# Forgetting heads that read their bias as loaded strips, and a top-k spread over the heads, in a hybrid decoder layer

## The chip, the cores and the metric

The kernel runs on one core of one Trainium2 chip. The metric is the device time of one execution in microseconds (us), as the median of the runs shown. PE is the tensor engine, PEld its weight loads, DVE the vector engine, ACT the scalar engine, POOL the GpSimd engine, and SP the engine whose queue issues most of the DMA transfers.

## The reference, cut

One layer over 512 positions of width 1024: a half-step SwiGLU block, then attention in two branches of 8 heads of 64, then a second half-step SwiGLU block. Branch A ("forgetting", heads 0 to 7) adds to its logits the difference of running sums of log-forget gates. Branch B ("sparse", heads 8 to 15) keeps, for each query, the 128 causal keys with the highest indexer scores. Both work in blocks of 128 queries.

```python
def fox_attention(q, k, v, log_f):
    cum = jnp.cumsum(log_f, axis=1).transpose(0, 2, 1)
    ...
        logits = jnp.einsum('bqhd,bkhd->bhqk', q[:, start:end], k[:, :end]).astype(jnp.float32) * scale
        logits = logits + cum[:, :, start:end, None] - cum[:, :, None, :end]
        logits = jnp.where(kpos <= qpos, logits, NEG_INF)
        p = jax.nn.softmax(logits, axis=-1).astype(v.dtype)
        outs.append(jnp.einsum('bhqk,bkhd->bqhd', p, v[:, :end]))

def dsa_attention(q, k, v, q_idx, k_idx, w_idx, rel_bias):
    ...
        score = jnp.einsum('bqhk,bqh->bqk', s_idx, w[:, start:end])
        score = jnp.where(causal[None], score, NEG_INF)
        _, sel = lax.top_k(score, topk)
        ...
        logits = logits + bias.transpose(0, 3, 1, 2)
        logits = jnp.where(valid[:, None], logits, NEG_INF)
        p = jax.nn.softmax(logits, axis=-1).astype(v.dtype)
```

## The kernel before

Every float32 operand of a large product is split into a high and a low half (tiles named h and l: wh and wl of weights, xh and xl of activations, ph and pl of softmax weights), and a product is three matmuls, or two where the halves of one side are stacked in one tile. `load_w` loads a weight tile over SP (ra, rb and rc in turn), ACT casts it to wh, and DVE subtracts it into wl.

The order of PE's instructions is the order of the code; that of the other engines is set by the compiler's scheduler, which fills gaps by its own estimates and keeps that order on each queue. The attention part stands in the middle of the kernel, between the two SwiGLU blocks. `Products` deals out projection matmuls (the units fk1, fq1, fv1 and so on) between the steps of the heads, by a fixed table FILL, so that PE always has work.

A head has four steps, s = 0 to 3, one query block each, the longest first: step s treats block i = 3 - s, with n = 128 (i + 1) keys. `softmax_block` takes the bias, lets PE form the logits (ps_qk, two banks of PSUM, with the scale's sign turned so that a minimum stands for a maximum), and DVE adds the bias and takes the minimum mn in one instruction (the line of `p<-ps_qk`). ACT takes the exponential and its sum, DVE the reciprocal rs, POOL scales p by it. `value_step`, which runs one head later, transposes p on PE (pt), splits it on ACT and DVE (ph, pl) and multiplies it with the values (po) one step after that.

For a forgetting head, `get_bias` loads the head's row of running sums (`cum_rows`, in DRAM), the same row to all 128 partitions, as one tile cb of 512 columns, of two in turn. For each block POOL makes a new tile b = cb - cum of the query (ncum, one value for each partition) and then sets the columns of the diagonal square that lie ahead of the query to 1e30. A sparse head's b is the selection (sc, 0 or 1e30) less a loaded table of relative positions.

The selection is made on DVE in `topk_steps`: 16 rounds over three score tiles (sc of 256, 384 and 512 columns), each a MAX of 8 values and a MATCH_REPLACE, and three last instructions; 99 steps in all. `topk_run(n)` adds n to a debt and takes a step for each whole unit. It is called after each small piece of projection ahead of the heads with TOPK_PRE, and twice in each block of the heads with TOPK_BEAT; at the end of head 7 what is left is taken at once. The tile sg holds small projections (forget logits, values and weights of the indexer) and cum the running sums.

Of the kernel before, what the change touches and what calls it, by code (L numbers as in the profile page):

```python
# [12 lines left out]
F32 = mybir.dt.float32  # L13
F32R = mybir.dt.float32r
AF = mybir.ActivationFunctionType
OP = mybir.AluOpType
# [3 lines left out]
P = 128  # L20
T = 512
NT = T // P
# [8 lines left out]
FILL_IX = 0.5  # L31
TOPK_PRE, TOPK_BEAT = 1.25, 1

# [3 lines left out]
H = 8  # L37
# [3 lines left out]
BIG = 1e30  # L41
S_W = 208
# [13 lines left out]
def tile_hybrid_layer(ctx: ExitStack, tc: tile.TileContext, a: dict):  # L56
    nc = tc.nc
    V, S, G, PE = nc.vector, nc.scalar, nc.gpsimd, nc.tensor
# [6 lines left out]
    small = ctx.enter_context(tc.tile_pool(name="small", bufs=4))  # L65
# [13 lines left out]
    for _ in range(WARM):  # L79
# [6 lines left out]
                    pattern=[[1, P]], channel_multiplier=-1)  # L86
    cpos = const.tile([P, P], F32, name="cpos")
# [781 lines left out]
    with (tc.tile_pool(name="mix", bufs=1) as mp, ExitStack() as att_ctx,  # L869
# [5 lines left out]
        kept = mp_dram.tile([P, 5, T], F32, name="kept")  # L875
        sg = at.tile([P, NT, S_W - 128], F32, name="sg")
        sd = [at.tile([P, NT, 2, DH], F32, tag="cb", bufs=2, name="sd") for _ in range(2)]
        dkh = at.tile([P, T], F32R, name="dkh")
        dkl = at.tile([P, T], F32R, name="dkl")
        dvv = at.tile([P, NT, P], F32R, name="dvv")  # L880
        cum = at.tile([P, NT, H], F32, name="cum")
        ncum = at.tile([P, NT, H], F32, name="ncum")
        dram = att_ctx.enter_context(tc.tile_pool(name="dram", bufs=1, space=bass.MemoryType.DRAM))
# [263 lines left out]
        def forget():  # L1147
# [25 lines left out]
            PE.matmul(pc[:, :NT * H], trin, lf.rearrange("p t h -> p (t h)"), start=True, stop=False)  # L1173
            PE.matmul(pc[:, :NT * H], ones, before.rearrange("p t h -> p (t h)"), start=False, stop=True)
            V.tensor_copy(cum, pc[:, :NT * H].rearrange("p (t h) -> p t h", t=NT))
            V.tensor_scalar(ncum, cum, -1.0, None, op0=OP.mult)
            yield
# [110 lines left out]
        def get_k(g):  # L1288
# [15 lines left out]
            return out  # L1304

        def get_bias(g):
            cb = at.tile([P, T], F32, tag="cb", bufs=2, name="cb")
            nc.sync.dma_start(cb, cum_rows[g:g + 1, :].to_broadcast([P, T]) if g < H else a["rel"][g - H])

            def bias(i):  # L1310
                n = P * (i + 1)
                b = tmp_tile("b")
                if g < H:
                    G.tensor_scalar(b[:, :n], cb[:, :n], 1.0, ncum[:, i, g:g + 1], op0=OP.mult, op1=OP.add)
                    G.affine_select(out=b[:, i * P:n], in_=b[:, i * P:n], compare_op=OP.is_ge, fill=BIG, base=0,
                                    pattern=[[-1, P]], channel_multiplier=1)
                else:
                    G.tensor_sub(b[:, :n], sc[i] if i else cpos, cb[:, T - n:T])
                return b[:, :n]
            return bias  # L1320
# [6 lines left out]
        for step in range(30):  # L1327
            prod.run(MM, upto["fv0"])
            topk_run(TOPK_PRE)
            if step == 5:  # L1330
                nk = get_k(0)
            if step == 10:
                next(later[1], 0)
            if step == 15:
                nq = get_q(0)
            if step == 24:
                nb = get_bias(0)
        prod.finish(upto["fv0"])
# [37 lines left out]
        for g in range(2 * H):  # L1376
            q, k, bias = nq, nk, nb
            probs[g] = [None] * NT
            st = [small.tile([P, NT], F32, tag=nm, name=nm) for nm in ("mn", "rs")]
            for s in range(NT):  # L1380
# [6 lines left out]
                if g + 1 < 2 * H:  # L1387
                    if s == 0:
                        nb = get_bias(g + 1)
                    if s == 0 and g % 2:  # L1390
                        nk = get_k(g + 1)
                    if s == 1 and g % 2:
                        nq = get_q(g + 1)
# [131 lines left out]
```

## Time and profile before

| | |
|---|---|
| runs, us | 1044.01, 1043.91, 1044.5; median 1044.01 |
| profiled execution, us | 1043.44, span 1041.7 |
| granted clock | 1.0 |
| DVE, ACT, POOL busy | 82%, 64%, 25% of the span |
| stretch with the forgetting heads | about 427 to 533 us |

An engine's busy time in a row of a stretch comes with the count of its instructions in brackets. In rows in order of time the first number is the start from the span's beginning, the second the length; a bracket at the end holds the idle time of the engine before the row and what ended it. SPq is SP's queue of transfers. Matmuls overlap: the next starts before the one ahead is over.

### The profile page before, as it was taken

The numbers are of one execution on the slowest core, as the hardware profiler recorded it, in microseconds if no ns is written. First come the engines' busy times: TensorE is split into PE (matmuls) and PEld (weight loads), VectorE is DVE, ScalarE is ACT, GpSimd is POOL, SyncE is SP. The second block draws the span as 40 slices with busy tenths as digits, with TensorE's granted clock in tenths as the row PEclk, the third lists the DMA queues.
The fourth block names the chain that finished last, engine by engine and source line by source line (L and its number), as shares of the span: only waits on it lengthen the run. The fifth ranks groups of instructions, "written<-read, shape, count | busy, mean of one in ns | idle before, by whom it ended". The sixth has DMA issues, their size and how long they took to land.

```text
span 1041.7 us, 19489 instructions
## 1 busy us (share of the span) xinstructions
PE 1027.9 (99%) x7424; PEld 960.6 (92%) x7424; DVE 851.7 (82%) x1405; ACT 668.8 (64%) x1118; POOL 256.6 (25%) x324
## 2 busy tenths in 40 slices
PE   9999999999999999999999999999999999999998
PEld 8889999999999999989887788888889999999998
DVE  6897888897989779977868765853987888988887
ACT  6547765865787765567767665433736865875783
POOL 1100111120121124285867552000100210111111
PEclk9999999999999999999999999999999999999999
DMA  7444755666567367633314311532553665567554
GB/s 257 108 152 120 158 161 132 150 163 175 124 142 185 113 166 190 182 97 93 86 57 132 119 54 52 181 112 81 131 164 96 146 150 177 129 162 192 131 128 132
DMA packets 57341, 142.66 MB, mean 137 GB/s; under 512 B 6424, under 2 KB 15768, under 8 KB 57248
## 3 DMA queue, kind: packets, MB, share of 16 engines
q1 hardware_dynamic: 39600, 110.21, 34.1%
q0 software_dynamic: 17504, 30.94, 16.6%
q8 instruction: 58, 0.95, 0.4%
q10 hardware_dynamic: 144, 0.27, 0.1%
q14 instruction: 35, 0.29, 0.1%
HBM read 104.94 MB, written 3.42 MB: 104 GB/s over the span
## 4 chain that ended last, share of the span: by engine, by line
PE 89%; DVE 5%; POOL 3%; issue 2%; DMA 1%; ACT 1%; POOLq 0%; DVEq 0%; ACTq 0%
PE pB L155 5%; PE pB L157 5%; PE pB L156 5%; PE ps_f L155 3%; PE pA L155 3%; PE pA L157 3%; PE pA L156 3%; PE ps_f L157 3%; PE ps_f L156 3%; PE dB L157 2%; PE dB L155 2%; PE dB L156 2%; PE ps_t L157 2%; PE ps_t L155 2%; PE ps_t L156 2%; PE dA L156 2%
## 5 line engine op out<-in xcount | busy, mean ns | idle before, releaser
L123 ACT CAST wh<-s 128x1024 fp32r<-128x1024 f32 (+1 forms) x90 | 86.8, 965 | 66.8 <-PE pC L156 31.5
L130 DVE TENSOR_TENSOR wl<-s,wh 128x1024 fp32r<-128x1024 f32 (+1 forms) x90 | 100.4, 1116 | 19.9 <-ACT wh L123 19.9
L155 PE MATMUL ps_t<-wh,xh 128*128 128x256 f32 (+1 forms) x288 | 81.2, 282 | 0.0
L157 PE MATMUL ps_t<-wh,xl 128*128 128x256 f32 (+1 forms) x288 | 80.4, 279 | 0.0
L156 PE MATMUL ps_t<-wl,xh 128*128 128x256 f32 (+1 forms) x288 | 80.3, 279 | 0.0
L155 PE MATMUL pB<-tbh,wh 128*128 128x256 f32 x288 | 79.5, 276 | 0.0
L156 PE MATMUL pB<-tbl,wh 128*128 128x256 f32 x288 | 79.5, 276 | 0.0
L157 PE MATMUL pB<-tbh,wl 128*128 128x256 f32 x288 | 79.5, 276 | 0.0
L249 POOL DMA_DIRECT2D b<-gu x12 | 10.4, 864 | 220.3 <-DVE rb L449 89.4
L155 PE MATMUL ps_f<-xh,wh 128*128 128x512 f32 (+1 forms) x152 | 59.0, 388 | 0.0
L157 PE MATMUL ps_f<-xh,wl 128*128 128x512 f32 (+1 forms) x152 | 57.9, 381 | 0.0
L156 PE MATMUL ps_f<-xl,wh 128*128 128x512 f32 (+1 forms) x152 | 57.7, 380 | 0.0
L1242 ACT ACTIVATE p<-p,mn 128x512 f32<-128x512 f32 (+1 forms) x64 | 36.1, 564 | 29.5 <-DVE mn L1240 29.2
L155 PEld LDWEIGHTS ps_t<-wh,xh 128*128 128x128 f32 x288 | 54.5, 189 | 0.5
L156 PEld LDWEIGHTS ps_t<-wl,xh 128*128 128x128 f32 x288 | 54.4, 189 | 0.5
L157 PEld LDWEIGHTS ps_t<-wh,xl 128*128 128x128 f32 x288 | 54.4, 189 | 0.2 <-DVE xl L168 0.2
L157 PEld LDWEIGHTS pB<-tbh,wl 128*128 128x128 f32 x288 | 54.1, 188 | 0.0
L156 PEld LDWEIGHTS pB<-tbl,wh 128*128 128x128 f32 x288 | 54.1, 188 | 0.0
L155 PEld LDWEIGHTS pB<-tbh,wh 128*128 128x128 f32 x288 | 54.1, 188 | 0.0
L1244 POOL TENSOR_SCALAR p<-p,rs 128x512 f32<-128x512 f32 (+1 forms) x64 | 39.2, 615 | 58.9 <-DVE rs L1243 53.5
L575 POOL DMA_DIRECT2D gx<-e x20 | 23.9, 1241 | 119.4 <-ACT wh L123 99.9
L1256 DVE TENSOR_TENSOR pl<-pt,ph 128x512 fp32r<-128x512 f32 (+1 forms) x64 | 31.0, 485 | 17.7 <-ACT ph L1255 17.5
(406 smaller groups left out, 4195.9 us busy)
## 6 DMA issues: line engine op xcount, KB each, us to landing
rf<-in_w_pair_dram SPq DMA_DIRECT2D x15, 512.0 KB, 4.1
rc<-in_w_pair_dram SPq DMA_DIRECT2D x12, 512.0 KB, 3.6
re<-in_w_pair_dram SPq DMA_DIRECT2D x12, 512.0 KB, 3.6
rd<-in_w_pair_dram SPq DMA_DIRECT2D x12, 512.0 KB, 4.0
rb<-in_w_pair_dram SPq DMA_DIRECT2D x12, 512.0 KB, 4.3
gx<-e POOLq DMA_DIRECT2D x22, 256.0 KB, 4.3
ra<-in_w_pair_dram SPq DMA_DIRECT2D x9, 512.0 KB, 3.8
rd<-in_w_halves_dram SPq DMA_DIRECT2D x12, 384.0 KB, 3.7
```

Source lines behind the costliest of these rows:

```text
L123: S.copy(wh[:, :f], raw[:, :f])
L130: V.tensor_sub(wl[:, :f], raw[:, :f], wh[:, :f].bitcast(F32))
L155: PE.matmul(out, lh, rh, start=start, stop=False, **more)
L156: PE.matmul(out, lh, rl, start=False, stop=False, **more)
L157: PE.matmul(out, ll, rh, start=False, stop=stop, **more)
L249: G.dma_start(l, src, accum_op=OP.add)
L575: G.dma_start(xa[:, d:d + 2, HT:], t["e"][part], accum_op=OP.add)
L1242: S.activation(p, p, AF.Exp, bias=mn, scale=-1.0, accum_out=rs)
L1244: G.tensor_scalar(p, p, rs, 1.0, op0=OP.mult, op1=OP.mult)
L1256: V.tensor_sub(pl[:, sl], pt[:, sl], ph[:, sl].bitcast(F32))
```

## The change

Four strips of running sums are loaded for each forgetting head, one for each block, 128 (i + 1) columns wide, and POOL writes the 1e30 into the diagonal square of the strip itself. DVE adds the strip to the logits as it is. The query's own sum is left out: it is one number for a whole row of logits, and the softmax does not change with it. So ncum and POOL's 32 subtractions are gone, and SP has 32 loads in the place of 8. Strips 3 and 2 take turns in the two cb buffers, strip 3 of the next head loaded at step 1 and strip 2 at step 2; strips 1 and 0 share one buffer (that of sg) and are loaded at step 0 of their own head. The top-k takes 1.1 and 0.25 steps a call in the place of 1.25 and 1.

```diff
--- before.py
+++ after.py
@@ -29,7 +29,7 @@
 FILL = (2.1, 2.3, 2.0, 2.0, 1.7, 1.7, 1.7, 1.7, 2.0, 2.0, 1.9, 1.9, 1.9, 1.9, 2.0, 2.2)
 FILL_LAST = 0.8
 FILL_IX = 0.5
-TOPK_PRE, TOPK_BEAT = 1.25, 1
+TOPK_PRE, TOPK_BEAT = 1.1, 0.25
 
 ADDING = range(6, 16)
 MM = 0.64
@@ -873,13 +873,11 @@
         rt = rb = None
         tn, fv, iq, pA, ga, gb = {}, {}, [], [], [], []
         kept = mp_dram.tile([P, 5, T], F32, name="kept")
-        sg = at.tile([P, NT, S_W - 128], F32, name="sg")
+        sg = at.tile([P, 3 * P], F32, tag="sg", name="sg")[:, :NT * (S_W - 128)].rearrange("p (t c) -> p t c", t=NT)
         sd = [at.tile([P, NT, 2, DH], F32, tag="cb", bufs=2, name="sd") for _ in range(2)]
         dkh = at.tile([P, T], F32R, name="dkh")
         dkl = at.tile([P, T], F32R, name="dkl")
         dvv = at.tile([P, NT, P], F32R, name="dvv")
-        cum = at.tile([P, NT, H], F32, name="cum")
-        ncum = at.tile([P, NT, H], F32, name="ncum")
         dram = att_ctx.enter_context(tc.tile_pool(name="dram", bufs=1, space=bass.MemoryType.DRAM))
         cum_rows = dram.tile([H, T], F32, name="cum_rows")
         wi = at.tile([P, NT, H], F32, name="wi")
@@ -1172,8 +1170,8 @@
             pc = psum.tile([P, T], F32, tag="pt", bufs=2, name="pc")
             PE.matmul(pc[:, :NT * H], trin, lf.rearrange("p t h -> p (t h)"), start=True, stop=False)
             PE.matmul(pc[:, :NT * H], ones, before.rearrange("p t h -> p (t h)"), start=False, stop=True)
+            cum = small.tile([P, NT, H], F32, tag="cr", bufs=1, name="cum")
             V.tensor_copy(cum, pc[:, :NT * H].rearrange("p (t h) -> p t h", t=NT))
-            V.tensor_scalar(ncum, cum, -1.0, None, op0=OP.mult)
             yield
             ps = psum.tile([P, T], F32, tag="pt", bufs=2, name="ps_ct")
             for t in range(NT):
@@ -1303,19 +1301,31 @@
                 out.append(k)
             return out
 
+        def causal_rows(g, i):
+            if i:
+                strip = at.tile([P, T] if i > 1 else [P, 3 * P], F32, tag="cb" if i > 1 else "sg",
+                                bufs=2 if i > 1 else 1, name="cb")
+            else:
+                strip = strips[1][:, 2 * P:]
+            n = P * (i + 1)
+            nc.sync.dma_start(strip[:, :n], cum_rows[g:g + 1, :n].to_broadcast([P, n]))
+            G.affine_select(out=strip[:, i * P:n], in_=strip[:, i * P:n], compare_op=OP.is_ge, fill=BIG, base=0,
+                            pattern=[[-1, P]], channel_multiplier=1)
+            strips[i] = strip
+
+        strips = {}
+
+        def forget_bias(i):
+            return strips[i][:, :P * (i + 1)]
+
         def get_bias(g):
             cb = at.tile([P, T], F32, tag="cb", bufs=2, name="cb")
-            nc.sync.dma_start(cb, cum_rows[g:g + 1, :].to_broadcast([P, T]) if g < H else a["rel"][g - H])
+            nc.sync.dma_start(cb, a["rel"][g - H])
 
             def bias(i):
                 n = P * (i + 1)
                 b = tmp_tile("b")
-                if g < H:
-                    G.tensor_scalar(b[:, :n], cb[:, :n], 1.0, ncum[:, i, g:g + 1], op0=OP.mult, op1=OP.add)
-                    G.affine_select(out=b[:, i * P:n], in_=b[:, i * P:n], compare_op=OP.is_ge, fill=BIG, base=0,
-                                    pattern=[[-1, P]], channel_multiplier=1)
-                else:
-                    G.tensor_sub(b[:, :n], sc[i] if i else cpos, cb[:, T - n:T])
+                G.tensor_sub(b[:, :n], sc[i] if i else cpos, cb[:, T - n:T])
                 return b[:, :n]
             return bias
 
@@ -1334,7 +1344,8 @@
             if step == 15:
                 nq = get_q(0)
             if step == 24:
-                nb = get_bias(0)
+                for i in (3, 2, 1, 0):
+                    causal_rows(0, i)
         prod.finish(upto["fv0"])
 
 
@@ -1374,7 +1385,7 @@
             return upto["dq1"] if g < 6 else upto["ga7"] if 4 * g + s < 4 * 9 + 2 else len(units)
 
         for g in range(2 * H):
-            q, k, bias = nq, nk, nb
+            q, k, bias = nq, nk, forget_bias if g < H else nb
             probs[g] = [None] * NT
             st = [small.tile([P, NT], F32, tag=nm, name=nm) for nm in ("mn", "rs")]
             for s in range(NT):
@@ -1385,8 +1396,14 @@
                 softmax_block(g, NT - 1 - s, q, k, bias, probs[g], st)
                 prod.run(FILL[g] / 2, limit(g, s))
                 if g + 1 < 2 * H:
-                    if s == 0:
+                    if s and g + 1 < H:
+                        for i in ((), (3,), (2,), ())[s]:
+                            causal_rows(g + 1, i)
+                    if s == 0 and g + 1 >= H:
                         nb = get_bias(g + 1)
+                    if s == 0 and 0 < g < H:
+                        for i in (1, 0):
+                            causal_rows(g, i)
                     if s == 0 and g % 2:
                         nk = get_k(g + 1)
                     if s == 1 and g % 2:
```

The scheduler sets a new order on DVE, ACT, POOL and SP; PE's is the same. In the rows below, p,mn<-ps_qk is the block's instruction, MAX and MATCH_REPLACE are top-k steps, fv belongs to the values, rs is a reciprocal, kl and st belong to the next heads' K and Q.

First place, DVE at head 0's first two blocks, before and now:

```order
L1014 SCALAR_TENSOR_TENSOR fv<-ps_t,rstd,fv 128x4x64
L1189 MAX m_5331<-sc_4155 128x8
L1191 MATCH_REPLACE sc_4154<-m_5310,sc_4154 128x384
L1189 MAX m_5354<-sc_4153 128x8
L1240 ISA p,mn<-ps_qk,b 128x512
L1240 ISA mn 128x1
L150 TENSOR_TENSOR wl<-rc,wh 128x1024
L1191 MATCH_REPLACE sc_4155<-m_5331,sc_4155 128x512
L1014 SCALAR_TENSOR_TENSOR fv<-ps_t,rstd,fv 128x4x64 x2
L1189 MAX m_5363<-sc_4154 128x8
L1191 MATCH_REPLACE sc_4153<-m_5354,sc_4153 128x256
L1240 ISA p,mn<-ps_qk,b 128x384
```

```order
L1012 SCALAR_TENSOR_TENSOR fv<-ps_t,rstd,fv 128x4x64 x2
L1238 ISA p,mn<-ps_qk,cb 128x512
L1238 ISA mn 128x1
L1189 MATCH_REPLACE sc_4151<-m_5378,sc_4151 128x256
L150 TENSOR_TENSOR wl<-rc,wh 128x1024
L1012 SCALAR_TENSOR_TENSOR fv<-ps_t,rstd,fv 128x4x64
L1241 RECIPROCAL rs<-rs 128x1
L1238 ISA p,mn<-ps_qk,cb 128x384
L1238 ISA mn 128x1
L1012 SCALAR_TENSOR_TENSOR fv<-ps_t,rstd,fv 128x4x64
```

Behind the first block stood four steps ahead of the second, and there are fewer in front of the first too; one is left between them.

Second place, DVE at the end of head 2 and the start of head 3 (the blocks of 128 and 512 columns), before and now:

```order
L1243 RECIPROCAL rs<-rs 128x1
L1240 ISA p,mn<-ps_qk,b 128x128
L1240 ISA mn 128x1
L1240 ISA p,mn<-ps_qk,b 128x512
L1240 ISA mn 128x1
L150 TENSOR_TENSOR wl<-rb,wh 128x1024
L1256 TENSOR_TENSOR pl<-pt,ph 128x128
L1243 RECIPROCAL rs<-rs 128x1 x2
```

```order
L1241 RECIPROCAL rs<-rs 128x1
L1254 TENSOR_TENSOR pl<-pt,ph 128x256
L1238 ISA p,mn<-ps_qk,cb 128x128
L1238 ISA mn 128x1
L896 TENSOR_SCALAR ss<-ss 128x8
L1241 RECIPROCAL rs<-rs 128x1
L1238 ISA p,mn<-ps_qk,cb 128x512
L1238 ISA mn 128x1
L150 TENSOR_TENSOR wl<-rb,wh 128x1024
L1189 MATCH_REPLACE sc_4151<-m_5940,sc_4151 128x256
L1254 TENSOR_TENSOR pl<-pt,ph 128x128
L1241 RECIPROCAL rs<-rs 128x1
```

The reciprocals of head 2's last blocks stood behind the split wl<-rb, two of them at once; now that of the block of 128 stands ahead of head 3's first block and of the split, and a replace stands behind the split.

Third place, DVE at the end of head 7, before from its block of 256 columns on, now from the row behind it:

```order
L1240 ISA p,mn<-ps_qk,b 128x256
L1240 ISA mn 128x1
L1276 TENSOR_TENSOR oAl<-o,oAh 64x512
L1240 ISA p,mn<-ps_qk,b 128x128
L1240 ISA mn 128x1
L1256 TENSOR_TENSOR pl<-pt,ph 128x256
L1243 RECIPROCAL rs<-rs 128x1 x2
L1036 TENSOR_TENSOR ga<-ps_f,rb 128x512
```

```order
L1187 MAX m_6910<-sc_4153 128x8
L1187 MAX m_6942<-sc_4151 128x8
L1187 MAX m_6945<-sc_4152 128x8
L1254 TENSOR_TENSOR pl<-pt,ph 128x384
L1274 TENSOR_TENSOR oAl<-o,oAh 64x512
L1189 MATCH_REPLACE sc_4153<-m_6910,sc_4153 128x512
L918 SCALAR_TENSOR_TENSOR st<-ps_q,gq,st 64x512
L1189 MATCH_REPLACE sc_4151<-m_6942,sc_4151 128x256
L1241 RECIPROCAL rs<-rs 128x1
L1189 MATCH_REPLACE sc_4152<-m_6945,sc_4152 128x384
L1254 TENSOR_TENSOR pl<-pt,ph 128x256
L1238 ISA p,mn<-ps_qk,cb 128x128
```

Three MAX now stand between the block and the next pl, and three MATCH_REPLACE ahead of the one behind that; the rest of the top-k (one MAX and replace and the three last instructions) follows behind the block of 128, ahead of head 8's first block.

## The prediction

> **What bounds the kernel now.** I read the page first, then busy time by stretch, then the rows of PE in order of time where it stood idle, then who had kept it waiting.
>
> ```profile
> span 1041.7 us, 19489 instructions
> PE 1027.9 (99%) x7424; PEld 960.6 (92%) x7424; DVE 851.7 (82%) x1405; ACT 668.8 (64%) x1118; POOL 256.6 (25%) x324
> PE 89%; DVE 5%; POOL 3%; issue 2%; DMA 1%; ACT 1%; POOLq 0%; DVEq 0%; ACTq 0%
> ...
> 427.00:457.00 30.00, 26.77 (x217) 25.63 (x216) 29.43 (x86) 19.74 (x41) 16.91 (x28) 1.00 0.43 131
> 457.00:533.00 76.00, 72.45 (x533) 67.63 (x532) 57.38 (x137) 57.02 (x128) 59.69 (x90) 1.00 0.29 85
> ```
>
> PE is busy for 99% of the span, so only PE's own holes can be won. The two stretches (columns: width, PE, PEld, DVE, ACT, POOL, clock, DMA share, GB/s) hold the eight forgetting heads: heads 0 and 1 in 427 to 457, heads 2 to 7 in 457 to 533. PE lacks 3.23 us in the first and 3.55 in the second. In the first DVE is full (29.43 of 30), in the second it has a quarter free. A softmax block goes PE logits, DVE sum with the bias and minimum, ACT exponential, DVE reciprocal, POOL scaling; four blocks later it goes PE transpose, ACT high half, DVE low half pl, PE product po. PE fills the time between with projections, so a late link costs it nothing until a transpose finds p unscaled or a po finds pl unmade. The holes one by one, with the idle time and what ended it in brackets:
>
> ```profile
> 442.11 0.66 PE L1251 MATMUL pt<-ident,p 128*128 128x128 f32 x4 [0.71 <-POOL p L1244]
> 447.12 0.55 PE L1251 MATMUL pt<-ident,p 128*128 128x128 f32 x3 [1.09 <-DVE pl L1256]
> 451.53 0.44 PE L1251 MATMUL pt<-ident,p 128*128 128x128 f32 x2 [0.77 <-DVE pl L1256]
> 455.84 0.39 PE L1262 MATMUL po<-pl,fv 128*128 128x256 f32 x1 [0.66 <-DVE pl L1256]
> 473.08 0.66 PE L1251 MATMUL pt<-ident,p 128*128 128x128 f32 x4 [1.43 <-POOL p L1244]
> 504.68 0.41 PE L1251 MATMUL pt<-ident,p 128*128 128x128 f32 x2 [0.62 <-DVE rs L1243]
> 513.64 0.50 PE L1261 MATMUL po<-ph,fv 128*128 128x512 f32 x1 [0.27 <-ACT o L1271]
> 520.23 0.39 PE L1262 MATMUL po<-pl,fv 128*128 128x256 f32 x1 [0.78 <-DVE pl L1256]
> 523.36 0.65 PE L1251 MATMUL pt<-ident,p 128*128 128x128 f32 x4 [0.23 <-POOL p L1244]
> ...
> 399.81 0.28 PE L156 MATMUL ps_t<-wl,xh 128*128 128x256 f32 x1
> 399.93 0.28 PE L157 MATMUL ps_t<-wh,xl 128*128 128x256 f32 x1
> ```
>
> The last two rows show that a busy matmul runs 0.28 us while the next starts 0.12 after it, so a hole costs about 0.16 more than its idle time. Four holes in the first stretch: 3.23 + 4 x 0.16 = 3.87 us. Five in the second: 3.33 + 0.80 = 4.13. About 8.0 us is all that this change can win on PE, whose own instructions stand in the same order before and after.
>
> **Fewer top-k steps in front.**
>
> ```profile
> 427.00:457.00 30.00, 14.68 (x40) 0.00 (x0) 1.00 0.43 131
> L1189 DVE MAX8 m<-sc x48: 408/562/723, 379.4 to 450.3; 128x8 f32<-128x256 f32 x16, 128x8 f32<-128x384 f32 x16, 128x8 f32<-128x512 f32 x16
> L1191 DVE MATCH_VALUE_LOAD sc<-m,sc x48: 64/86/121, 380.9 to 453.1; 128x8 f32 x48
> L1191 DVE MATCH_REPLACE8 sc<-m,sc x48: 399/552/719, 380.9 to 453.2; 128x256 f32<-128x256 f32 x16, 128x384 f32<-128x384 f32 x16, 128x512 f32<-128x512 f32 x16
> ...
> 427.56 0.40 PE L929 MATMUL ps_qk<-kl,st 128*128 128x512 f32 x1
> 430.51 0.68 DVE L1240 CUSTOM_DVE_ANT_0 p<-ps_qk,b 128x512 f32<-128x512 f32 x1
> ```
>
> The first row is the same stretch for the tile sc alone: 14.68 us of DVE's 29.43 are top-k. A step is a MAX (0.56) or a load and replace (0.09 + 0.55), 0.60 in the mean. Head 0's first logits are there at 427.96; DVE comes to them at 430.51, 2.55 late, and the holes at 447, 451 and 455 still wait for its pl. In the rows of order of the first place, and counted on, 78 of the 99 steps stood ahead of the first softmax block and all 99 ahead of the ninth block; now it is 73 and 77. So 22 steps x 0.60 = 13.2 us leave a stretch in which DVE was some 2.5 us late, and it needs about 16 us of 30 (29.43 - 13.2). The reciprocals of head 0, which stood two and three steps behind their exponentials, then reach POOL blocks ahead of the transpose at 442. All four holes should close: I take 3.8. Ends: 3.87, and 2.0 if a late weight load holds ACT and DVE instead (below).
>
> Of the 22 steps, 11 now lie singly in blocks 10 to 30 and 11 in a lump. The single ones, 11 x 0.6 = 6.6 us, enter a DVE that is 75% busy (57.38 of 76). Most fall into its idle time; I charge 0.8, one more hole like that at 520.23, between 0 and 4.
>
> The lump (third place) stands on both sides of head 7's last block, because the sparse heads' bias needs the finished selection. Rows for it:
>
> ```profile
> 527.18 0.27 PE L929 MATMUL ps_qk<-kl,st 128*128 128x256 f32 x1
> 529.75 0.34 PE L1262 MATMUL po<-pl,fv 128*128 128x384 f32 x1
> 532.74 0.39 PE L1262 MATMUL po<-pl,fv 128*128 128x256 f32 x1
> ...
> L1240 DVE CUSTOM_DVE_ANT_0 p<-ps_qk,b 128x512 f32<-128x512 f32 (+3 forms) x32 | 15.5, 486 | 3.4 <-POOL b L1315 2.8 <-PE ps_qk L929 0.2
> L1256 DVE TENSOR_TENSOR pl<-pt,ph 128x512 fp32r<-128x512 f32 (+3 forms) x27 | 13.2, 489 | 3.6 <-ACT ph L1255 3.5
> L1276 DVE TENSOR_TENSOR oAl<-o,oAh 64x512 fp32r<-64x512 f32 x6 | 6.3, 1047 | 0.1
> L920 DVE SCALAR_TENSOR_TENSOR st<-ps_q,gq,st 64x512 fp32r<-64x512 f32 x8 | 6.0, 750 | 1.1 <-ACT st L919 0.9
> L1318 POOL TENSOR_TENSOR b<-sc,cb x24: 738/1021/2286, 527.4 to 626.3; 128x512 f32<-128x512 f32 x8, 128x384 f32<-128x384 f32 x8, 128x256 f32<-128x256 f32 x8
> ```
>
> Walk it in before's times: logits ready at 527.45, block 0.58 (to 528.03), three MAX 1.69 (529.7), pl 0.49 (530.2): PE wanted that pl at 529.75, 0.5 late. Then oAl 1.05, replace 0.64, st 0.75, replace 0.64, rs 0.16, replace 0.64, pl 0.49: 534.6, where PE, itself 0.5 late, wants it at 533.2: 1.4 late. After the last step POOL forms the bias of head 8's first block (1.0 to 1.3) with DVE waiting for it; two banks for logits cover that but for some 0.1. I charge 2.0, between 0 (the scheduler's order fits the gaps) and 3.5 (the bias wait comes through whole).
>
> **Loaded strips instead of a bias made on POOL.**
>
> ```profile
> L1314 POOL TENSOR_SCALAR b<-cb,ncum x32: 368/539/1543, 425.3 to 527.0; 128x512 f32<-128x512 f32 x8, 128x384 f32<-128x384 f32 x8, 128x256 f32<-128x256 f32 x8, 128x128 f32<-128x128 f32 x8
> 437.92 1.22 DVE L150 TENSOR_TENSOR wl<-ra,wh 128x1024 fp32r<-128x1024 f32 x1
> 469.87 2.42 DVE L150 TENSOR_TENSOR wl<-rb,wh 128x1024 fp32r<-128x1024 f32 x1
> 470.15 1.04 POOL L1004 TENSOR_TENSOR kn<-kn,rh 128x512 f32<-128x512 f32 x1
> 472.65 1.05 POOL L1244 TENSOR_SCALAR p<-p,rs 128x128 f32<-128x128 f32 x2 [1.45 <-DVE rs L1243]
> ```
>
> POOL loses 32 x 0.54 = 17 us and keeps its 32 selections; DVE no longer waits 2.8 us for them (the row of L1240 above). The hole at 473.08 is a p that POOL could not scale since its reciprocal stood behind a wl of 2.42 us, twice the usual 1.22, while POOL worked on kn and other tiles behind its biases. In the new order (second place) that reciprocal stands ahead of the wl: 1.43 + 0.16 = 1.59 back. The one at 523.36 waits for POOL alone: 0.39 back. Of 520.23 I take half (0.47), of 504.68 the bias part (0.2), of 513.64 nothing, since it waits for ACT. Sum 2.65, between 0 and 4.13.
>
> [...]
>
> What the strips add: SP issues 32 loads for 8.
>
> ```profile
> DMA to landing us min/median/max: 2.5/3.1/5.9
> 456.06 0.39 PE L928 MATMUL ps_qk<-kh,st 128*128 128x512 f32 x1
> 520.45 0.39 PE L928 MATMUL ps_qk<-kh,st 128*128 128x512 f32 x1
> 421.05 0.38 SPq L143 DMA_DIRECT2D rc<-in_w_fq_dram  x1
> 427.23 1.05 ACT L144 CAST wh<-rc 128x1024 fp32r<-128x1024 f32 x1 [2.29 <-PE ps_t L157]
> ```
>
> Five heads take 64.4 us, so a head 12.9 and a block 3.2. Strips 3 and 2 are reloaded one head ahead. Strips 1 and 0 share a buffer that is free after block 0 of the head before and needed three blocks later, 9.6 us; issue 0.4, landing at most 5.9 and a selection of 0.3 to 0.6 make 6.9. So the loads cost nothing, with 2.7 us of cover; if that is used up DVE waits in its queue and with it the reciprocals, p, ph and pl. In front the weights rc now pass behind three more issues, some 1.4 us later, and ACT's cast perhaps 1 later; the DVE time just freed covers it. For every second head SP also carries the copies that double a K tile; one kl copy now stands behind strip 2 of the next head and waits for block 2 of the present one. It is needed at the next head's first logits, two blocks or 6.4 us later, and a landing of 3.1 fits, one of 5.9 just. The extra bytes, 128 x (512 + 384 + 256 + 128 - 512) x 4 for each of eight heads, 3.1 MB, meet a DMA share of 0.29 to 0.43. The removed sign change of the sums, one DVE instruction, lay ahead of both stretches: nothing.
>
> **Sum.** -3.8 - 2.65 + 0.8 + 2.0 = -3.65 us against the profiled execution's 1043.44 (span 1041.7 and 1.7 around it): 1039.8. The runs' median, 1044.01, lies 0.57 above it, so 1040.4.
>
> **Rivals.** (1) No change: the wait moves. The single steps cost 4 and the lump 3.5: -6.45 + 7.5 = +1.05, 1045.1. For it: DVE was what kept PE in three of the first four holes, and 13 us of it only move. Against: the quarter of DVE that is free. 0.15. (2) More: POOL's removed work also frees wl and oAl, all nine holes close and the lump hides: -8.0, 1036.0. For it: 2.42 against 1.22; against: the ACT hole and the walk. 0.15. (3) Slower: strips come late. Strips 1 and 0 stand on SP behind weight loads that wait for DVE; if that wait passes the 2.7 us of cover by 1 us in each of seven heads, it is -3.65 + 7 = +3.35, 1047.4. Against: each of those loads waits for a split that DVE does well ahead of the block that frees the strip. 0.10.
>
> **Numbers.** The forecast has 0.60, with its own range 1038.5 to 1042.5. A measurement of this kernel tells 0.2% from no change: 1041.9 and 1046.1. Faster takes 0.50 of the forecast's 0.60, all of (2) and a little of (1): 0.67. Same: 0.10 of the forecast and most of (1): 0.22. Slower: (3) and a remainder: 0.11. The range 1036.0 to 1044.5 leaves out (3), the upper part of (1) and a sliver below.
>
> **What would show it.** Right: no PE hole over 0.3 us between 427 and 457, DVE about 55% busy there, POOL's bias rows gone, DVE waiting for strips nowhere, and one or two new holes of about 0.5 and 1.4 us at PE's po between head 7's third block and head 8's first. Wrong: DVE's block rows waiting for POOL's selections or a DMA in each head, or holes of the first kind recurring in heads 2 to 7.

## The result and the profile after

The change makes the kernel slower: 1050.09 us (six runs, 1048.55 to 1053.19) against 1044.07 for the kernel before beside it (six runs, 1043.2 to 1044.5), a ratio of 1.0065, 95% interval 1.0053 to 1.0076. The prediction was 1040.4, in a range of 1036.0 to 1044.5. The profiled execution took 1049.91 us (span 1048.2), 6.5 more than that of before.

First the page (share of the span and count of instructions in each engine), then the two stretches of the prediction, with the same columns as there.

```profile
span 1048.2 us, 19498 instructions
PE 1030.0 (98%) x7424; PEld 963.0 (92%) x7424; DVE 848.9 (81%) x1404; ACT 669.0 (64%) x1118; POOL 240.9 (23%) x292
...
427.00:457.00 30.00, 27.25 (x224) 26.53 (x224) 20.46 (x52) 19.72 (x42) 14.16 (x21) 1.00 0.58 172
457.00:533.00 76.00, 69.48 (x503) 65.70 (x502) 56.30 (x142) 54.35 (x120) 44.01 (x62) 0.96 0.40 116
```

DVE and POOL did get the relief: DVE 20.46 of 30 us for 29.43, POOL 44.01 of 76 for 59.69. PE has the same 7424 matmuls, 2.1 us longer in sum; it still lacks 2.75 us in the first stretch and now 6.52 in the second (3.55 before), and the second shows a granted clock of 0.96. PE's rows over 0.2 us of idle time, with what ended it in brackets:

```profile
436.75 0.33 PE L926 MATMUL ps_qk<-kh,st 128*128 128x128 f32 x1 [1.15 <-DVE mn L1238]
448.27 0.52 PE L1249 MATMUL pt<-ident,p 128*128 128x128 f32 x3 [1.60 <-DVE pl L1254]
465.55 0.44 PE L1260 MATMUL po<-pl,fv 128*128 128x384 f32 x1 [0.56 <-DVE pl L1254]
479.84 0.41 PE L1249 MATMUL pt<-ident,p 128*128 128x128 f32 x2 [1.05 <-DVE pl L1254]
500.97 0.52 PE L1249 MATMUL pt<-ident,p 128*128 128x128 f32 x3 [0.50 <-DVE pl L1254]
505.16 0.41 PE L1249 MATMUL pt<-ident,p 128*128 128x128 f32 x2 [1.24 <-DVE pl L1254]
513.89 1.11 PE L1249 MATMUL pt<-ident,p 128*128 128x128 f32 x4 [3.16 <-POOL p L1242]
535.21 0.44 PE L1260 MATMUL po<-pl,fv 128*128 128x384 f32 x1 [0.60 <-DVE pl L1254]
539.10 0.38 PE L1260 MATMUL po<-pl,fv 128*128 128x256 f32 x1 [0.93 <-DVE pl L1254]
542.31 0.66 PE L1249 MATMUL pt<-ident,p 128*128 128x128 f32 x4 [0.29 <-POOL p L1242]
```

One hole stands out, 3.16 us at 513.89. Around it, us by us, PE's busy time (second number) and the granted clock (the 0.97, 0.50, 0.62 after the five engines):

```profile
512.00:513.00 1.00, 0.00 (x0) 0.00 (x0) 0.00 (x0) 0.00 (x0) 0.00 (x0) 0.97 0.98 345
513.00:514.00 1.00, 0.11 (x1) 0.11 (x2) 0.00 (x0) 0.00 (x0) 0.81 (x3) 0.50 0.29 109
518.00:519.00 1.00, 1.00 (x6) 1.00 (x6) 0.86 (x2) 0.03 (x1) 0.89 (x2) 0.50 0.63 137
519.00:520.00 1.00, 1.00 (x7) 0.95 (x6) 0.00 (x0) 0.06 (x1) 1.00 (x1) 0.62 0.17 42
```

The clock is halved from 512.94 (0.97 is 0.06 us at one half) to 519.76 (0.62 is 0.76 us), 6.8 us. PE starts 6 or 7 matmuls in a microsecond there, for 9 to 11 between 506 and 510, while counting as fully busy: this loss stands in no hole. PE was at work for 5.9 of those 6.8 us, which at half speed costs 2.9. Row by row it is a little less: from those transposes to the logits two blocks of work later PE took 6.33 us (513.89 to 520.22), for 4.06 before (510.14 to 514.20) with a hole of 0.43 in it, so 2.7 more.

The account against before, each hole with 0.16 for its start as in the prediction: first stretch 3.07 for 3.87 (-0.8); the hole at 513.89, 3.32; the clock behind it, 2.7 to 2.9; the other holes up to 533, 3.99 for 4.13 (-0.1); those at 535 to 542, 2.30, for one of 0.97 at 558.54 of before that is gone (+1.3). Together 6.4 to 6.6, where 6.5 were measured. So the loss is one hole and the clock behind it, and the question is besides why the 8 us of old holes were merely replaced.

What made the hole is in POOL's rows. L1312 is the selection of a strip, L1242 the scaling of p; SP's rows (L1311 loads a strip) stand below them.

```profile
507.25 0.48 POOL L1242 TENSOR_SCALAR p<-p,rs 128x256 f32<-128x256 f32 x1 [1.63 <-DVE rs L1241]
511.61 0.29 POOL L1312 TENSOR_SCALAR_AFFINE_SELECT cb<-cb 128x128 f32<-128x128 f32 x1 [3.88 <-DMA cb<-cum_rows]
513.19 0.29 POOL L1312 TENSOR_SCALAR_AFFINE_SELECT cb<-cb 128x128 f32<-128x128 f32 x1 [1.29 <-DMA cb<-cum_rows]
513.47 1.04 POOL L1242 TENSOR_SCALAR p<-p,rs 128x128 f32<-128x128 f32 x2
...
507.87 0.80 SPq L1311 DMA_DIRECT2D cb<-cum_rows  x2
```

The scheduler put the selections of head 6's strips 1 and 0 ahead of the scaling of head 5's last block. Their shared buffer is freed by that same block on DVE, so the loads can only go out at 507.87, and the second lands at 513.13. POOL stood idle for 5.2 us (3.88 + 1.29), and the scaling stood ready behind the selections from 509.02, when its reciprocal on DVE was done, to 513.47; the transposes at 513.89 wait for the scaling. In the order of POOL's instructions this was to be seen without a run:

```
 TENSOR_SCALAR p<-p,rs 128x256
 AFFINE_SELECT cb<-cb 128x128 x2
 TENSOR_SCALAR p<-p,rs 128x128
```

In front, the weights of the next projection are late. Rows of ACT and DVE in order of time, and of the view of loads (KB each, us from issue to landing):

```profile
432.40 1.05 ACT L144 CAST wh<-rc 128x1024 fp32r<-128x1024 f32 x1 [5.03 <-DMA rc<-in_w_fq_dram]
435.14 0.72 ACT L1240 ACTIVATE p<-p,mn 128x512 f32<-128x512 f32 x1
...
433.48 1.23 DVE L150 TENSOR_TENSOR wl<-rc,wh 128x1024 fp32r<-128x1024 f32 x1 [4.12 <-ACT wh L144]
...
rc<-in_w_fq_dram SPq DMA_DIRECT2D x1, 512.0 KB, 9.0
```

ACT sat 5.03 us before the cast; before, the same cast began at 427.23 and waited for PE. The exponential of head 0's first block stands behind it on ACT, and DVE waits 4.12 us for the cast. The freed time of DVE is there, but as waiting. Hence the holes at 436.75 and 448.27, in place of the four of before.

### The profile page after: what moved, and what is told of

It reads as the page before. It is cut to its first block, busy times and chain, and to the rows that moved or that the text cites. A ratio compares the mean times of both kernels' runs of the same rounds, so it can differ in the third digit from the quotient of the medians.

```text
span 1048.2 us, 19498 instructions
## 1 busy us (share of the span) xinstructions
PE 1030.0 (98%) x7424; PEld 963.0 (92%) x7424; DVE 848.9 (81%) x1404; ACT 669.0 (64%) x1118; POOL 240.9 (23%) x292
## 3 DMA queue, kind: packets, MB, share of 16 engines
HBM read 108.09 MB, written 3.42 MB: 106 GB/s over the span
## 4 chain that ended last, share of the span: by engine, by line
PE 85%; DVE 7%; ACT 3%; issue 2%; DMA 2%; POOL 0%; SPq 0%; POOLq 0%; ACTq 0%; DVEq 0%
PE pB L155 5%; PE pB L156 5%; PE pB L157 5%; PE pA L155 3%; PE pA L156 3%; PE pA L157 3%; PE ps_f L155 3%; PE ps_f L156 3%; PE ps_f L157 3%; PE dB L157 2%; PE dB L155 2%; PE dB L156 2%; PE dA L156 2%; PE pD L155 2%; PE pC L155 2%
## 5 line engine op out<-in xcount | busy, mean ns | idle before, releaser
L1242 POOL TENSOR_SCALAR p<-p,rs 128x512 f32<-128x512 f32 (+1 forms) x64 | 37.3, 585 | 50.4 <-DVE rs L1241 50.2
```

The source lines that it names most:

```text
L1242: G.tensor_scalar(p, p, rs, 1.0, op0=OP.mult, op1=OP.mult)
```

## The experiments

Times are differences to the kernel before in the same set of runs (medians 1043.37, 1043.17 and 1043.12 there); the changed kernel stands at +6.0.

**The constants alone.**

```diff
 before.py
-TOPK_PRE, TOPK_BEAT = 1.25, 1
+TOPK_PRE, TOPK_BEAT = 1.1, 0.25
```

> The kernel before with the two constants alone (1.1 and 0.25): the bias is still made on POOL, the strips are absent. Theory S (the strips make the change slow: in the profile after, two selections stand on POOL ahead of head 5's last scaling, and PE loses 3.32 us at 513.89 and 2.8 us to a halved clock behind it): without strips none of this can happen, and the constants bring what the prediction's first term and its two charges say, -3.8 + 0.8 + 2.0 = -1.0, so 1043 us, between 1041 and 1045; PE's hole at 513 is under 0.5 us. Theory K (the top-k steps that moved into the heads make it slow, and the hole at 513.89 is only where it shows): about 1050, 5 us or more above the kernel before.

1042.88 us, -0.5, ratio 0.9996 (0.9987 to 1.0004). The same two stretches:

```profile
427.00:457.00 30.00, 30.00 (x250) 29.66 (x249) 23.88 (x61) 21.10 (x45) 16.91 (x24) 1.00 0.39 127
457.00:533.00 76.00, 69.78 (x506) 64.73 (x505) 63.24 (x154) 55.76 (x126) 58.51 (x86) 1.00 0.27 81
```

PE has no hole left in the first stretch (30.00) and lacks 6.22 in the second, 2.7 more than before. Nothing falls to the clock. That is what theory S says.

**The strips alone.**

```diff
 after.py
-TOPK_PRE, TOPK_BEAT = 1.1, 0.25
+TOPK_PRE, TOPK_BEAT = 1.25, 1
```

> The changed kernel with the two constants of before (1.25 and 1): strips alone. Theory S: slower than before by 2 to 8 us (1046 to 1052); on POOL's order selections of strips 1 and 0 stand ahead of the scaling of head 0's and of head 1's last block here, not of head 5's, so PE's holes should lie near 442 and 456 and not at 513. Theory K: no slower than before, 1041 to 1044, as the prediction's third term (-2.65) says.

1051.98 us, +8.6, ratio 1.0077 (1.0063 to 1.009). The holes lay at the scalings where the order put them (head 0's last block, at 449.49, and, 0.79 us only, head 1's at 465.99; 7 and 10 us later than expected, behind the late front, whose own hole is the first row) and at one place that was not expected:

```profile
438.51 0.33 PE L926 MATMUL ps_qk<-kh,st 128*128 128x128 f32 x1 [2.29 <-DVE mn L1238]
449.49 1.11 PE L1249 MATMUL pt<-ident,p 128*128 128x128 f32 x4 [4.73 <-POOL p L1242]
520.31 1.12 PE L1249 MATMUL pt<-ident,p 128*128 128x128 f32 x4 [3.19 <-POOL p L1242]
...
518.21 0.29 POOL L1312 TENSOR_SCALAR_AFFINE_SELECT cb<-cb 128x128 f32<-128x128 f32 x1 [3.76 <-DMA cb<-cum_rows]
```

The hole at 520.31 is that of 513.89 again: I had read its order as free of it, and it was not. The strips are the cause, with either pair of constants.

**Selections behind the scaling.** The scheduler is told to issue the selection of strips 1 and 0 after the scaling of the head before.

```diff
 after.py
+            scaled[g, i] = G.tensor_scalar(p, p, rs, 1.0, op0=OP.mult, op1=OP.mult)
...
+            with tc.issue_after(scaled[g - 1, 0].ins) if g and i < 2 else nullcontext():
+                G.affine_select(out=strip[:, i * P:n], in_=strip[:, i * P:n], ...)
```

> The changed kernel with the selections of strips 1 and 0 of a head held in POOL's order behind the scaling of the last block of the head before. Against the changed kernel this moves two places on POOL (heads 1 and 5) and nothing on PE, DVE, ACT or SP. Theory S with the clock: the hole at 513.89 (3.32 us) goes and with it the 2.8 us that PE lost at the halved clock behind it: 6.1 us less, 1044 us, and PE's clock is 1.00 through 513 to 520. Theory S without the clock (the clock falls there for another reason): 3.3 less, 1046.7, and the clock still falls. Rival (the strips themselves come too late for DVE's blocks, POOL's order only shows it first): the hole moves to the next block and the time stays above 1048.

1045.24 us, +1.9, ratio 1.0016 (1.0007 to 1.0025). POOL now (the scaling ahead, the selection still waiting, for nobody's loss):

```profile
511.42 0.38 POOL L1242 TENSOR_SCALAR p<-p,rs 128x128 f32<-128x128 f32 x1 [1.39 <-DVE rs L1241]
513.77 0.30 POOL L1313 TENSOR_SCALAR_AFFINE_SELECT cb<-cb 128x128 f32<-128x128 f32 x1 [1.97 <-DMA cb<-cum_rows]
...
510.00:522.00 12.00, 12.00 (x84) 10.98 (x83) 9.96 (x29) 9.69 (x25) 6.91 (x11) 1.00 0.35 100
```

PE is busy without a break from 510 to 522, at full clock. Two places in POOL's order are worth 4.9 us between the medians, 4.1 if each is set against its own runs of before, where 6.1 were expected; in this profile the front hole had grown to 1.81 us and the clock fell there instead (below).

**Two strips fewer in front.**

```diff
 after.py
-                for i in (3, 2, 1, 0):
+                for i in (3, 2):
                     causal_rows(0, i)
...
-                    if s == 0 and 0 < g < H:
+                    if s == 0 and g < H:
                         for i in (1, 0):
                             causal_rows(g, i)
```

> The changed kernel with only strips 3 and 2 of head 0 loaded in front; strips 1 and 0 are asked for inside head 0, so that the weights rc of w_fq stand ahead of them on SP. Theory F (four strip loads ahead of those weights make them land 9.0 us after their issue, ACT's cast waits 5.0 us and everything behind it on ACT): the weights land 2 to 4 us sooner, ACT's wait falls under 3 us, the hole at 436.75 (1.32 us) goes and that at 448.27 (1.79) shrinks: 1.3 to 3 us less, 1047 to 1049. Rival (the landing is long for another reason, such as the other loads already under way): ACT's wait and both holes stay, 1050. Both leave the hole at 513.89 and the clock behind it where they are.

1047.45 us, +4.1, ratio 1.0037 (1.0025 to 1.005): 1.9 us of the 6.0. The weights land 6.8 us after their issue, where it was 9.0:

```profile
430.12 1.05 ACT L144 CAST wh<-rc 128x1024 fp32r<-128x1024 f32 x1 [2.62 <-DMA rc<-in_w_fq_dram]
446.11 0.52 PE L1249 MATMUL pt<-ident,p 128*128 128x128 f32 x3 [0.74 <-DVE pl L1254]
511.79 0.66 PE L1249 MATMUL pt<-ident,p 128*128 128x128 f32 x4 [3.04 <-POOL p L1242]
```

The first front hole is gone, the second halved, that of POOL untouched: theory F. Not all of the 1.9 need be the front's: in this profile the clock behind POOL's hole is halved for 3.4 us (513.37 to 516.78), where it was 6.8 in that of the changed kernel.

**Both edits.** The two diffs above together.

> The changed kernel with both edits of the experiments above together: selections of strips 1 and 0 held behind the scaling of the head before, and strips 1 and 0 of head 0 asked for inside head 0. If the two causes are separate, the gains add: 4.9 (selections) + 2.6 (front) off the changed kernel's 1050.1 give 1042.6, between 1041.5 and 1043.7; no PE hole over 1.5 us stays and the clock is 1.00 throughout 427 to 545. If they share one cause, the second edit brings under 1 us: 1044.5 to 1045.5.

1042.63 us, -0.5, ratio 0.9994 (0.9986 to 1.0003). Against before the two gains were 4.1 and 1.9, and together they are 6.5: two causes, and they account for the whole 6.0. The clock stays at 1.00 in both stretches. But a hole of 1.25 us at 524.67 and the lump's remain, and the kernel is level with the constants alone.

**Steps out of the heads.** Top-k rounds 13 to 16 are left out, so none is left for the heads.

```diff
 both edits
-            for r in range(TOPK // 8):
+            for r in range(TOPK // 8 - 4):
```

> As the kernel with both edits, but four of the sixteen rounds of the top-k are left out (24 steps, so that the mask keeps fewer keys): with the constants 1.1 and 0.25 no step is then left for the heads. What it gains on the kernel with both edits is the price of the steps inside the heads. By the prediction's charges (0.8 for those that lie singly, 2.0 for the lump) it gains 2.8: about 1039.8. If the holes that wait for DVE's pl in heads 2 to 7 are all the steps' doing (465, 479, 500 and 505 of the changed kernel, 4.2 us, and the lump's 2.5), it gains 6 to 7: 1036. If they come from the weights' splits and the copies that DVE has anyway, it gains 2.5 or less and the holes near 479 and 505 stay.

1038.91 us, -4.3, ratio 0.9965 (0.9953 to 0.9978): 3.7 under the kernel with both edits, where the prediction's charges were 2.8. Of the holes near 479, 500 and 505 of the changed kernel those at 476.16 (0.62), 497.51 (0.51) and 501.21 (0.73) stay, so these are only partly the steps' doing.

**No lump.**

```diff
 both edits
-TOPK_PRE, TOPK_BEAT = 1.1, 0.25
+TOPK_PRE, TOPK_BEAT = 1.1, 0.5
```

> As the kernel with both edits, with TOPK_BEAT 0.5 for 0.25: one step in each block, so that the selection ends before head 7 and no lump is left. If the lump costs its 2.0 to 2.5 (holes at 535, 539 and 542 of the changed kernel) and a step by itself next to nothing, it gains 1.5 to 2.5 on the kernel with both edits: 1040.5. If what counts is the number of steps in a crowded DVE, not where they lie, it comes out within 0.7 of that kernel.

1041.38 us, -1.8, ratio 0.9981 (0.9973 to 0.999): 1.25 better than with 0.25, less than the lump's 2.3. The holes do not show why: the profiled execution was the fastest of the eleven (1038.94) and has, beside the lump's, that of 1.25 us gone, with those at 477 and 499 at 1.21 and 1.17 us for 1.07 and 0.51 with both edits. That the single steps cost something where DVE is crowded fits the last two, and is not shown for the median.

**One load per head, selected in place.** Blocks run from the longest to the shortest, so the square of block i - 1 can be overwritten in the same tile once block i has read it.

```diff
 after.py
         def causal_rows(g, i):
+            if i == NT - 1:
+                strips[g] = at.tile([P, T], F32, tag="cb", bufs=2, name="cb")
+                nc.sync.dma_start(strips[g], cum_rows[g:g + 1, :].to_broadcast([P, T]))
+            own = strips[g][:, i * P:(i + 1) * P]
+            G.affine_select(out=own, in_=own, ...)
...
+            if g < H and i:                # in softmax_block, behind DVE's sum
+                causal_rows(g, i - 1)
```

> The changed kernel with one load per head as before, of 512 columns, and the four diagonal blocks selected in place one after the other, each after the block that still reads it unmasked: 8 loads instead of 32, 32 selections, no bias made on POOL, the same two constants. Theory S says that everything wrong came from the loads (their queueing ahead of the weights in front, and POOL waiting for them): the prediction's sum then holds as it stands, -3.65, 1040 us, and no selection waits for a DMA except the first of each head. Rival (the relief of POOL is worth nothing on PE's path): it comes out with the kernel that has the constants alone, -0.5, 1042.9.

1042.74 us, -0.4, ratio 0.9994 (0.9985 to 1.0003). It has 8 loads again, but one of them repeats the fault on a small scale; the row below is POOL's, and PE's hole follows it:

```profile
509.30 0.29 POOL L1311 TENSOR_SCALAR_AFFINE_SELECT cb<-cb 128x128 f32<-128x128 f32 x1 [4.13 <-DMA cb<-cum_rows]
510.00 0.65 PE L1251 MATMUL pt<-ident,p 128*128 128x128 f32 x4 [1.71 <-POOL p L1244]
```

So the number agrees with the rival for another reason than the rival's, and this run by itself does not decide.

**In place, behind the scaling, no lump.**

```diff
 in place
-TOPK_PRE, TOPK_BEAT = 1.1, 0.25
+TOPK_PRE, TOPK_BEAT = 1.1, 0.5
...
+            with tc.issue_after(scaled[g - 1, 3].ins) if g and i == 3 else nullcontext():
+                G.affine_select(out=own, in_=own, ...)
```

> The kernel with one load per head and selections in place, and two further edits: the first selection of a head (the one that waits for its load) is held in POOL's order behind the scaling of the present head's first block, and TOPK_BEAT is 0.5. In the first in-place kernel that selection stood once ahead of head 5's last scaling (hole of 1.88 us at 510.00), and its lump cost 0.77 + 1.08 + 0.46. If both go, 1042.7 - 1.9 - 2.3 = 1038.5, or some 1 us above that for the steps that now lie singly: 1038.5 to 1040, under every kernel so far. If the holes only move to the next crowded place on DVE (477, 499, 503), it stays at 1041.4, the time of the kernel with both edits and 0.5.

1039.02 us (1038.78 to 1039.51), -4.1, ratio 0.9961 (0.9949 to 0.9974): faster than both kernels and than all others that do the whole work.

```profile
427.00:457.00 30.00, 29.63 (x246) 29.11 (x245) 23.42 (x63) 21.48 (x45) 13.23 (x24) 1.00 0.41 133
457.00:533.00 76.00, 72.95 (x528) 67.83 (x527) 62.08 (x161) 58.41 (x131) 48.79 (x65) 1.00 0.28 84
L1312 POOL TENSOR_SCALAR_AFFINE_SELECT cb<-cb 128x128 f32<-128x128 f32 x21 | 8.5, 409 | 3.8 <-DVE mn L1238 3.7
...
427.48 1.05 ACT L144 CAST wh<-rc 128x1024 fp32r<-128x1024 f32 x1 [2.29 <-PE ps_t L157]
```

The selections (third row: busy, mean ns, then the idle time before them and its cause) wait for DVE's block and for no load, and the cast in front waits for PE, with the very 2.29 us of before.

**The other constants with the bias on POOL.**

```diff
 before.py
-TOPK_PRE, TOPK_BEAT = 1.25, 1
+TOPK_PRE, TOPK_BEAT = 1.1, 0.5
```

> The kernel before with the two constants 1.1 and 0.5 and nothing else. It prices the strips against a bias made on POOL, at the same constants: the kernel with both edits and 0.5 had 1041.4. If the relief of POOL is worth the prediction's 2.65 there, this one has 1044; if it is worth nothing, this one has 1041 to 1042 too.

1044.61 us, +1.5, ratio 1.0014 (1.0005 to 1.0023). With the same constants the strips in good order are 3.2 us faster (1041.38, another set of runs) and the strips in place 5.6. At 0.25 the strips with both edits bring nothing (-0.5 against -0.5). Here two holes of 1.70 and 1.73 us, at 471.66 and 506.41, lie behind a late DVE: the first waits for a scaling whose reciprocal ended at 471.14, the second for DVE itself. Ahead of the first, DVE's block of 256 had waited 1.20 us for its bias on POOL and a wl had taken 1.97 us beside POOL's kn. So the biases did stand in the way there; but the kernels differ in the order of every engine but PE, and how much of the 3.2 and 5.6 us is POOL's relief is not shown.

**A hole by hand, without strips.** On POOL the scaling of head 5's last block is held up by extra scalings by one.

```diff
 before.py
+            for _ in range(12 if (g, i) == (5, 0) else 0):      # 7 in the second kernel
+                G.tensor_scalar(p, p, 1.0, 1.0, op0=OP.mult, op1=OP.mult)
             G.tensor_scalar(p, p, rs, 1.0, op0=OP.mult, op1=OP.mult)
```

> The kernel before with twelve extra scalings by one (128x128, 0.38 us each, 4.6 us) on POOL ahead of the scaling of head 5's last block. No strip is in it. The scaling has some 1.4 us to spare, so PE waits about 3.2 us once, as at 513.89 of the changed kernel. Theory C (a long hole brings the clock down, whatever made it): PE's clock is 0.50 for 3 to 7 us behind the hole and the time rises by the hole and 1.5 to 2.9 us more: 4.7 to 6.1. Rival (the clock fell in the changed kernel for a reason of its own, its transfers or the other engines' work): the time rises by the hole alone, 3.2, and the clock is 1.00.

> The same with seven extra scalings (2.7 us), so that the hole is about 1.3 us. Theory C with a threshold (the fall was seen behind holes of 1.81 and of 3.0 us and more, not behind 1.43 and 1.60): the time rises by 1.3 and the clock stays at 1.00. If any hole costs clock in proportion: 1.3 + 1 and a clock under 1.00 for a while.

Twelve: 1049.69 us, +6.6, ratio 1.0061 (1.0048 to 1.0074). Seven: 1045.95, +2.8, ratio 1.0027 (1.0016 to 1.0038). The scaling had 0.5 us to spare in the kernel before (done at 509.63, PE there at 510.14) and not 1.4, and the scheduler put head 6's first scaling (0.69 us) ahead of it too, with twelve also one of POOL's `rh` (1.65). So the holes became 5.95 and 2.64 us; the first two rows are of the kernel with twelve, the rest of that with seven.

```profile
515.74 1.11 PE L1253 MATMUL pt<-ident,p 128*128 128x128 f32 x4 [5.95 <-POOL p L1246]
516.00:520.00 4.00, 4.00 (x19) 4.00 (x19) 1.33 (x4) 2.45 (x5) 3.48 (x6) 0.50 0.01 4
...
512.70 0.66 PE L1253 MATMUL pt<-ident,p 128*128 128x128 f32 x4 [2.64 <-POOL p L1246]
514.00:515.00 1.00, 1.00 (x8) 1.00 (x7) 0.69 (x1) 0.98 (x2) 1.00 (x1) 0.63 0.09 25
515.00:516.00 1.00, 1.00 (x7) 1.00 (x6) 0.00 (x0) 0.17 (x1) 1.00 (x4) 0.50 0.00 0
517.00:518.00 1.00, 1.00 (x5) 0.86 (x5) 0.05 (x1) 0.48 (x1) 1.00 (x2) 0.67 0.00 0
```

The halved clock needs no strip: a POOL-made wait brings it down in the kernel before too, with few transfers under way (a DMA share of 0.17 from 509.80 to the fall at 513.27, 0.01 in the second row, for 0.59 from 509.5 to 513 in the changed kernel). The small case that was meant, a hole of 1.3 us, did not come about, and neither total is the sum of hole and clock (5.95 and 2.64 us of idle time, plus half of the 4.4 and 3.4 us that PE worked at the halved clock): the engines that PE waits for catch up meanwhile, and later holes close (those at 513.64 and 523.36 of before are gone in both, that at 520.23 in the first).

## Why the prediction was wrong, point by point

- **Where the time can be won**: right. PE's holes decided every comparison; POOL's busy time fell by 15.7 us for the 17 worked out, the top-k's in the first stretch by 12.0 for 13.2 (14.68 to 2.69; other work filled part of it, so DVE was 68% busy there and not 55%), and both told nothing of the time.
- **First term, -3.8 for the top-k steps that leave the front**: right by itself. With the constants alone all four holes close. The step that failed is the sentence that the late weights cost nothing because the DVE time just freed covers them. The lateness was taken as 1.4 us behind three issues plus 1 of the cast; measured were an issue 2.3 us later (423.32 for 421.05), a landing of 9.0 us for the 5.5 of before, and 5.03 us of ACT waiting. The cover was the wrong engine's, too: the cast holds ACT, and with it head 0's exponential, which DVE then waits for. The named lower end, a gain of only 2.0 "if a late weight load holds ACT and DVE instead", was the case, and worse: 0.8.
- **0.8 for single steps and 2.0 for the lump**: about right. The constants alone cost 2.7 us in the second stretch, leaving the steps out brought 3.7. The lump's holes were predicted as about 0.5 and 1.4 at po near head 7/8 and came as 0.60 and 0.93 there, with 0.29 at the next transpose.
- **-2.65 for POOL's subtractions**: the named hole at 473.08 did go, but others, at 479.84, 500.97 and 505.16 (2.79 us), wait for DVE's pl, and 4.13 became 3.99. The term was a sum over the holes that were there, without those that open in a new order. The changed kernel's 3.99 also holds the single top-k steps; with the strips alone the holes there besides POOL's long one came to 3.31 (0.79, 0.61, 0.51 and 0.76 us and 4 x 0.16), so in that order 0.8 of the 2.65 was left (1.8 without the 0.79, which a strip's selection made). In a better order it may be more: strips in place are 5.6 us faster than POOL's bias at the same constants, though how much of that is POOL's relief is not shown.
- **Strips at no cost, "2.7 us of cover"**: the step that lost the case. The cover was counted from the release of the buffer to DVE's need for the strip, and held: DVE's blocks waited 0.5 us in all for selections by the profile (3.9 more are put down to other work of POOL). What was not asked is who stands behind the selection on POOL, a scaling that is needed much earlier than the strip. The prediction did ask this of SP's queue and of DVE's, and let POOL keep "its 32 selections".
- **By term**: the first came out 3.0 us short, the strips at 3.3 for the hole and 2.7 to 2.9 for the clock where nothing was charged, the single steps and POOL's relief together at -0.1 for -1.85, the lump at +1.3 for 2.0.
- **Rival (3), late strips**: the right sign at 0.10, by the wrong mechanism. It charged 1 us in each of seven heads; it was 3.32 us in one head, by POOL's queue, and what it left out entirely is the clock. Of its signs that it is wrong, "DVE's block rows waiting for POOL's selections" did not show; "holes of the first kind recurring" did.
- **Rival (2), more**: a part of what it expected showed. POOL was busy for 44.01 us of the second stretch, for 59.69 before, and DVE's oAl took 769 ns there for 1047:

```profile
L1274 DVE TENSOR_TENSOR oAl<-o,oAh 64x512 fp32r<-64x512 f32 x5 | 3.8, 769 | 0.4 <-ACT oAh L1273 0.4
```

  Most of that difference is one instruction, the oAl at 517.21 of before, which took 2.57 us while POOL worked on p, kn and b; the other five of before took 0.67 to 0.86, the five of the changed kernel 0.67 to 1.12. How much of it is POOL's relief is not shown. PE's other holes there stayed at 3.99 us for 4.13.
- **The clock**: not in the prediction at all, and 2.7 to 2.9 us of the 6.5.

## What to carry to other kernels

When an operation that must wait for a load is put on an in-order queue, count what stands behind it on that queue (here a scaling that was ready at 509.02 and ran at 513.47), not only who needs its result; the written order shows it before any run. A buffer whose release and whose next load hang on the same block makes the whole latency of the load (here 5.2 us) a wait for whatever is queued behind it, and a tile that can be changed in place needs no such load. Price a long hole on PE at more than its length (here 3.16 us, and 2.7 to 2.9 of halved clock behind it), and don't cover one engine's lateness with another's free time without following the queue.

## What the hardware showed beyond that

The granted clock falls by half behind some holes and not behind others, for 3.4 us or 6.8. In the kernel with the selections behind the scaling it fell behind a hole of 1.81 us (its end is at 438.68), in that with the strips alone it did not behind one of 2.29 (the third row; its hole is at 438.51):

```profile
439.00:440.00 1.00, 1.00 (x10) 1.00 (x9) 0.62 (x5) 0.37 (x2) 0.57 (x2) 0.86 0.54 210
443.00:444.00 1.00, 1.00 (x9) 0.90 (x9) 0.44 (x4) 0.94 (x3) 0.59 (x2) 0.93 0.15 37
439.00:444.00 5.00, 5.00 (x43) 4.91 (x43) 5.00 (x18) 2.90 (x10) 2.07 (x4) 1.00 0.23 68
```

The first two rows put that fall at 439.72 (0.86) and its end at 443.14 (0.93): 3.42 us. Read in the same way, it is 6.82 in the changed kernel and 3.40 with seven extra scalings (514.26 to 517.66). The clock also fell at holes of 3.04 us (two strips fewer), 4.73 (strips alone) and 5.95 (twelve extra scalings), and it stayed at 1.00 at those of 1.70 and 1.73 (bias on POOL with 1.1 and 0.5) and of 1.71 (in place). The length of a hole does not tell the two kinds apart by itself, since that of 2.29 is longer than that of 1.81; what else decides is not shown.

The same kernel can scatter by the clock: the six runs of the changed kernel have mean clocks of 0.994 to 0.998 and span 4.6 us, those with 0.994 and 0.995 being the two longest, while the in-place kernel with 0.5 (clock 1.000 in all five) spans 0.7. With seven extra scalings the three runs at 1.000 took 1045.30 to 1045.45 us, the four at 0.998 took 1045.95 to 1046.91. It is not the only source of scatter: with both edits the runs span 3.1 us, at 0.998 to 1.000.

In the rows of the front the time of a load goes by what stands ahead of it more than by its size: in the changed kernel the strip of 256 KB, issued first, took 3.7 us from issue to landing, that of 64 KB, the last of the four, 8.3, and they landed in the order of issue with the 512 KB of weights behind them, which took 9.0; the next 512 KB of rc, issued at 434.74, took 3.7.
